# Projection, mask and tile work moved within their steps, and the attention half of the output weights split late

## The chip, the cores and the metric

The kernel runs on one core of a Trainium2 chip. The metric is the device time of one execution in microseconds (us); a measurement gives the median of several runs. The engines are named as the profile names them: PE (matrix multiply; PEld is its weight load), DVE (vector), ACT (scalar), POOL (GpSimd), SP (the queue that issues nearly all DMA transfers here). Each engine works through its own list of instructions in order.

## The reference

One layer of an encoder, for a prompt of 256 tokens and a sample of 2048 tokens (T = 2304 in all), width 1024, all in float32:

```python
h = rms_norm(x, g_pre)
q, k, v, z_a, u_f, z_f = split(h @ w_in)                  # six blocks of 512 columns
y_a = neighbourhood_attention(q, k, v, rpb)               # 8 heads of 64, windows of 8 x 16 cells in rows of 64
y_f = real(fft2(u_f, axes=(seq, group), norm='ortho')) @ w_f + b_f   # 8 groups of 64
mixed = concat([rms_norm(y_a, g_na) * silu(z_a), rms_norm(y_f, g_f) * silu(z_f)])
out = mixed @ w_out
return x + rms_norm(out, g_post)
```

The attention window of a token is clipped at the grid's borders; a table `rpb` gives a bias for each relative place, and what lies outside the window is masked.

## The kernel before, in words

**Products.** Each float32 matrix is split into a high part, rounded to the PE's format, and a low part, the rest. A product is then three matmuls: high by high, high by low, low by high (`mm3`, lines 159 to 162). A split is a pair of instructions: ACT makes the high part, and DVE (sometimes POOL) subtracts it to get the low part, so the low part waits for the high one.

**Stages.** (1) The first projections, v and u of the prompt and of a part of the sample. (2) Sixteen tiles b = 0 to 15 of the prompt's other projections (loop at line 756). (3) `vu(0, ...)`: v and u for the first half of the sample, by a fast multiplication scheme of seven products j = 0 to 6 per tile. (4) Eight pairs of weight blocks, i = 0 to 7, seven products j each (the loop at line 835; one step j is twelve matmuls). (5) `vu(1, ...)`, at i = 8, and i = 8 to 15 for the second half of the sample; along with it the first Fourier stage of u (`u_load`, `u_split`, `u_stage1`). (6) The rest of the Fourier transform. (7) The attention loop, steps k = 2 to 36 (line 1595), over 36 groups G[k]: four head pairs `pr` of nine groups `i` each; and with it the Fourier half of the output product. (8) The attention half of the output product, a loop over 18 token tiles (line 1757).

**What sets the order.** From stage 1 to 5, and again from the Fourier products on, the order of the instructions on every engine is the order of the program text (`manual_schedule`); each engine and the SP queue take them one after another. DMA transfers go through eight completion semaphores in turn, so that a transfer is issued only when the eighth one before it has landed.

**Around the places that are touched.**

- `n_first(j)` (line 425) splits an operand of 128 x 2048 of the scheme's right side; `op_split(j)` (line 466) splits four half tiles of its left side, v's and u's weights. In stage 2 they were called at b = 12, 13 and at b = 14, 15.
- In stage 4 and 5, each step j first prepares weights for the next pair (`w_load`, `w_sums` on POOL, `a_split` on ACT and DVE; what `a_split(i + 1, j)` makes is read seven steps later), then did `n_load`, `n_scale`, `n_diff` (operands for the second half), then `u_load`, `u_split`, `u_stage1`, and then runs the step's twelve matmuls.
- In step k of the attention loop, `scores(g)` puts the scores of G[k] into PSUM; `bias_max` (DVE) adds the bias and takes the extreme; `exps` (ACT) takes the exponential; `soft` (POOL) scales by the reciprocal sum. One step later `transp(f, b)` turns the weights on PE, in two calls b = 0 and 1: it writes two PSUM banks `ptb`, and ACT copies the one, DVE the other to SBUF (`pt`). The second call can only write when both copies of the first have been made. `pv(f)` multiplies by v. `f_mm(k)` is the Fourier half of the output product (PSUM tiles `po`), which `f_evac(k)` takes out into a tile `ofs`, on DVE for even k, on ACT for odd k, and stores to `oD` after the odd one. `split_q(G[k + 1])` (ACT, then POOL) splits the next queries, loaded into `ql` by `prep(G[k + 3])` at the end of step k. `mask_p` (POOL) masks the bias table of the next head pair's first group.
- The attention half of the output weights, `A["wo"][0]`, four blocks of 128 x 1024, is scaled by `gmix` and split. `wo_load` and `wo_split` (lines 701 to 711) did this within `vu(1, ...)` and stored both parts to a tensor `woD` in device memory; steps 24 to 31 of the attention loop loaded the eight results into `WO` (line 1616), which step 36 and stage 8 read.
- The pool behind `gt(...)` (tag `g`) has 13 buffers of 4 KB a partition. In the attention loop eight of them hold the Fourier half of the output weights (`wo1`) until step 35; the others serve `ofs`, and now `wor`.

The lines that order a step of the attention loop, behind the second call of `transp`:

```python
        if g:
            f_mm(k, range(6, 12))
        ...
        if pr < 3 and i == 8:
            mask_p(pr + 1)
        if k % 2 and x < 18:
            ys_split(ftiles[x])
        ...
        if g:
            f_evac(k)
        if f:
            pv(f)
```

Of the kernel before, what the change touches and what calls it, by code (L numbers as in the profile page):

```python
# [164 lines left out]
def build(tc, A, O):  # L165
# [18 lines left out]
    ivD = dr.tile([18, 128], F32, name="ivD")  # L184
    oD = dr.tile([T, D], F32, name="oD")
    yD = dr.tile([2, 4, 128, T], F32, name="yD")
    woD = dr.tile([2, 4, 128, D], F32, name="woD")
    tD = [dr.tile([4, 128, 2, 80 * n], F32, name="tD%d" % n) for n in (11, 15, 12)]

    ident = cst.tile([128, 128], F32, name="ident")  # L190
# [39 lines left out]
    def load(shape, src, name):  # L230
        t = gt(shape, F32, name)
        nc.sync.dma_start(t, src)
        return t
# [464 lines left out]
    for c in range(3):  # L698
        vu_out("u", c)

    def wo_load(x):
        wor[x] = load((128, D), A["wo"][0, x], "wr")

    def wo_split(x):
        w = wor.pop(x)
        g = gmix[:, x:x + 1]
        o = k8(F32R, "wo", (128, 2, D))
        nc.scalar.activation(o[:, 0], w, AF.Copy, scale=g)
        nc.vector.scalar_tensor_tensor(out=o[:, 1], in0=w, scalar=g, in1=f_(o[:, 0]), op0=ALU.mult, op1=ALU.subtract)
        for y in range(2):  # L710
            nc.sync.dma_start(woD[y, x], f_(o[:, y]))

    wor = {}
    for c in range(3, 6):
        if c == 3:
            iv_get(0, 2)
# [39 lines left out]
    for b in range(16):  # L756
        kind, blk = divmod(b, 4)
        if 1 <= b < 10:
            wz_load(1)
        if b == 2:  # L760
            n_load((1, 1))
        if b in (5, 7):
            r_put(b // 2 + 1)
        if b == 10:
            op_load(0)
        if b == 12:
            op_load(1)
        if 2 <= b < 14:
            b_raw(b + 2)
        if 2 <= b < 8:  # L770
            x, y = divmod(b, 2)
            n_scale(None, *divmod(x, 2)[::-1], range(2 * y, 2 * y + 2))
        elif 8 <= b < 12:
            n_sum(b - 8)
        if b in (5, 12, 13):
            n_first((5, 12, 13).index(b) + 1)
        if b > 13:
            op_split(b - 14)
        p = mmt(512)[:, :TP]
        wh, wl = wb.pop(b)  # L780
        for k in range(KC):
            mm3(nc, p, wh[:, k], wl[:, k], hp_[:, k], lp_[:, k], k == 0, k == KC - 1)
        o = st.tile([128, 256], F32, tag="f", name="f", bufs=3)
        if kind % 2:
            i, d = p, o
        else:
            i = p.rearrange("p (b r c) -> p b r c", b=2, c=32)
            d = o.rearrange("p (r b c) -> p b r c", b=2, c=32)
        nc.scalar.activation(d, i, AF.Silu if kind < 2 else AF.Copy)
        if kind < 2:  # L790
            nc.sync.dma_start(zD[kind, blk * 128:blk * 128 + 128, :TP], o)
        else:
            nc.sync.dma_start((kD if kind == 2 else qD)[blk, :, :TP], o)
# [14 lines left out]
    def at(i, f, *a):  # L808
        hooks.setdefault(i, []).append(call(f, *a))

    for x in range(4, 7):
        at(3 * x - 12, n_first, x)
    for x in range(4):
        at(2 * x + 1, rows_load, x + 5)
        at(2 * x + 4, rows_square, x + 5)
# [19 lines left out]
    for i in range(16):  # L835
        sg, pr = divmod(i, 8)
        if i == 8:
            hooks.clear()
            for x in (5, 6):
                at(2 * x - 9, b_split, x)  # L840
            for x in range(4):
                if x:
                    at(4 * x, wo_load, x)
                at(4 * x + 5, wo_split, x)
            at(20, w_load, 8)
            at(24, w_sums, 8)
            for j in range(7):
                at(24 + j // 2, a_split, 8, j)
            vu(1, range(4), hooks)
# [32 lines left out]

        silu_ = [None]
        for j in range(7):
            if i in (0, 8):
                if j in (0, 3):
                    w_load(i + 1 + j // 3)
                if i == 0 and j == 0:
                    a_split(0, 6)
                if i == 0 and j == 1:  # L890
                    row_scales(10, 8)
                if i == 0 and j == 4:
                    iv_rows(10, 8)
                    iv_put(10, 8)
                if i == 0 and j == 6:
                    iv_get(10, 8)
                if j == 2:
                    w_sums(i + 1)
                for x in {3: (0, 1), 4: (2, 3), 5: (4, 5), 6: (6,)}.get(j, ()):
                    a_split(i + 1, x)  # L900
            elif i not in (7, 15):
                if j == 0:
                    w_sums(i + 1)
                a_split(i + 1, j)
                if j == 3 and i < 14 and i != 6:
                    w_load(i + 2)
            elif i == 7:
                if j in (3, 4):
                    op_load(j - 3)
                if j in (5, 6):  # L910
                    op_split(j - 5)
                if j == 5:
                    wo_load(0)
            if sg == 0:
                x, y = divmod(7 * (pr - 1) + j, 14)
                if x in (0, 1):
                    if y == 0:
                        n_load(x)
                    elif 3 <= y < 7:
                        n_scale(x, *divmod(y - 3, 2))  # L920
                    elif 7 <= y < 12:
                        n_diff(x, y - 7)
                if pr == 6 and j in (2, 5):
                    (b_split if j > 2 else b_get)(0)
                if pr == 7 and j:
                    b_get(j)
                    if j > 2:
                        b_split(j - 2)
            if i == 2 and j == 0:
                for t, n in ((gmix, "gmix"), (bfs, "bf"), (dnyq, "dnyq"), (rmask, "rmask"), (csm, "csmask")):  # L930
                    nc.sync.dma_start(t, A[n])
                nc.sync.dma_start(cm, A["cmask"].rearrange("p (b x) -> p b x", b=2))
            for f, d in ((u_load, 0), (u_split, 4), (u_stage1, 6)):
                x = 7 * pr + j - 7 - d
                if sg and 0 <= x < 38 and x % 7 in (2, 4, 6):
                    f(x // 7 * 3 + x % 7 // 2 - 1)
            if i == 5 or 8 <= i < 15:
                t_step(max(0, i - 7), j)
            if i == 15 and j in (1, 3, 4, 5):
                if j == 1:  # L940
                    d2 = [load_d(0), load_d(1)]
                else:
                    zgs.append(load_z(j - 3))
            if 9 <= i < 15 and j == 2:
                v_copy(i - 9)
            p = mmt(512)
            aw = aop[i, j]
            bh, bl = bnew[sg, j]
            for k in range(4):
                mm3(nc, p, aw[:, 0, k], aw[:, 1, k], bh[:, k], bl[:, k], k == 0, k == 3)  # L950
            add = lambda o, u: nc.vector.tensor_tensor(out=e_(o), in0=uu[u], in1=p, op=ALU.add)
            if j == 0:
                nc.scalar.copy(e_("u0"), p)
            elif j == 1:
                comb(0, 0, "u0", p)
            elif j == 2:
                add("u2", "u0")
            elif j == 3:
                add("u4", "u2")
            elif j == 4:  # L960
                comb(1, 1, "u4", p)
                add("u3", "u2")
            elif j == 5:
                comb(1, 0, "u3", p, ALU.subtract)
                store(1)
            else:
                comb(0, 1, "u4", p)
                store(0)
# [596 lines left out]
        if R is None or hc:  # L1565
            nc.sync.dma_start(yD[0, pr, :, ts], y)

    WO = []

    NT = {4: range(2, 4), 8: range(4, 8), 10: range(8, 12), 11: range(12, 16), 12: range(16, 18),  # L1570
          32: range(4), 34: range(4, 8), 36: range(8, 12)}
# [23 lines left out]
    for k in range(2, len(G) + 1):  # L1595
# [12 lines left out]
            load_t(pr, 2)  # L1608
        if k == 9:
            nc.sync.dma_start(gpb, pbc(A["gpost"]))  # L1610
        if k == 23:
            wp = pt.enter_context(tc.tile_pool(name="wp", bufs=1, side="right"))
            WO.extend(wp.tile([128, 4, D], F32R, name="w0%d" % x) for x in range(2))
        if 24 <= k < 32:
            y = k - 24
            nc.sync.dma_start(WO[y % 2][:, y // 2].bitcast(F32), woD[y % 2, y // 2])
        x = k // 2 + 1
        if g:
            scores(g)
# [24 lines left out]
        if g:  # L1644
            if k + 1 < len(G):
                split_q(G[k + 1])
            soft(g, 1)
            if k == 2:
                ys_mul(ftiles[x])
                ys_load(ftiles[x + 1])  # L1650
# [5 lines left out]
            f_mm(k, range(6, 12))  # L1656
        else:
            a_mm(atiles[0], 1, range(6))
        if pr < 3 and i == 8:
            mask_p(pr + 1)  # L1660
        if k % 2 and x < 18:
            ys_split(ftiles[x])
        if pr < 3 and i in (5, 6, 7, 8):
            split_k(KK[pr + 1], i - 5)
        if k == 34:
            ys_split(atiles[0])
        if g:
            f_evac(k)
        if f:
            pv(f)  # L1670
        if k + 1 in NT:
# [15 lines left out]
        if k in (34, 35):  # L1687
            ys_load(atiles[k - 33])
            of_load(atiles[k - 34])
        if k == 36:  # L1690
            ys_split(atiles[1])


    def evac(d, p, ns, q):
# [110 lines left out]
```

## Time and profile before

| | us |
|---|---|
| median of 3 runs | 967.51 (967.21 to 969.06) |
| the profiled execution, its own time | 968.71 |
| span in that profile, first to last instruction | 966.9 |
| PE busy | 957.0 (99% of the span) |
| DVE busy | 710.4 (73%) |
| ACT busy | 496.2 (51%) |
| POOL busy | 429.8 (44%) |
| mean granted TensorE clock | 0.997 |

A row of a timeline has the start and the duration in us, the engine, the line, the operation, out<-in, shapes and the count of instructions merged into it; in brackets stands how long the engine had been idle, and what ended that. A row of the chain of waits has start, duration, and the work that the end of the program depended on. A matmul's duration is longer than the time until the next one may start, since matmuls are pipelined: the distance of the starts tells whether PE waited. The table of stages gives for each stretch its length, and for each engine its busy time with the number of instructions, then the granted clock, the DMA engines' busy share and GB/s.

### The profile page before, as it was taken

How to read it: one execution, taken by the hardware profiler on the slowest of the kernel's cores; microseconds unless marked ns; L12 is line 12 of the kernel's file. 1: busy time of each engine (PE TensorE's matmuls, PEld its weight loads, DVE VectorE, ACT ScalarE, POOL GpSimd, SP SyncE). 2: the span in 40 equal slices, each digit the busy share in tenths (PEclk: the TensorE clock that was granted, in tenths of full speed). 3: DMA queues.
4: the chain of work that ended last, by engine and by line, in shares of the span. 5: the costliest groups of instructions: out<-in, count | busy, mean ns of one | idle time of the engine just before them, and what ended most of it. 6: DMA issues, size and time to landing. Idle time of an engine off the chain costs nothing.

```text
span 966.9 us, 16988 instructions
## 1 busy us (share of the span) xinstructions
PE 957.0 (99%) x5743; PEld 798.7 (83%) x5743; DVE 710.4 (73%) x1310; ACT 496.2 (51%) x1077; POOL 429.8 (44%) x400
## 2 busy tenths in 40 slices
PE   9999999999999999999999999999999999999997
PEld 8889988888888888888887889787787887778886
DVE  6758978687886855798887358776666656649997
ACT  5845676423335432233344267676676766644443
POOL 2200002455752202665655044567677786524544
PEclk9999999999999999999999999999999999999998
DMA  8899696557748893599888895698877998979993
GB/s 304 323 359 374 243 347 244 194 189 276 292 189 358 293 352 117 193 386 335 294 308 319 292 346 208 197 278 280 267 234 245 273 312 260 281 255 333 342 341 130
DMA packets 140942, 269.81 MB, mean 279 GB/s; under 512 B 13402, under 2 KB 81840, under 8 KB 137464
## 3 DMA queue, kind: packets, MB, share of 16 engines
q1 hardware_dynamic: 140360, 268.32, 79.9%
q8 instruction: 46, 0.75, 0.3%
q10 hardware_dynamic: 432, 0.39, 0.1%
q14 instruction: 40, 0.33, 0.1%
q0 software_dynamic: 64, 0.02, 0.0%
HBM read 179.00 MB, written 96.81 MB: 285 GB/s over the span
## 4 chain that ended last, share of the span: by engine, by line
PE 92%; DMA 3%; DVE 1%; SPq 1%; ACT 1%; issue 1%; POOL 1%; DVEq 0%; ACTq 0%; POOLq 0%
PE po L1454 18%; PE mm L161 18%; PE mm L160 17%; PE mm L162 17%; PE pv L1543 5%; PE ptb L1527 5%; PE s L1185 4%; PE pab L1022 2%; DMA wr<-wz 1%; PE py L160 1%; PE py L162 1%; PE py L161 1%; DMA za<-zD 1%; DMA gpre<-gpre 0%; SPq L1153 0%
## 5 line engine op out<-in xcount | busy, mean ns | idle before, releaser
L160 PE MATMUL mm<-xh,wa 128*128 128x512 f32 x448 | 174.4, 389 | 0.0
L162 PE MATMUL mm<-xh,wa 128*128 128x512 f32 x448 | 174.3, 389 | 0.0
L161 PE MATMUL mm<-xl,wa 128*128 128x512 f32 x448 | 174.3, 389 | 0.0
L532 POOL TENSOR_TENSOR ws<-wr 128x512 f32<-128x512 f32 x16 | 23.3, 1455 | 219.9 <-DMA wr<-wz 207.1
L1219 POOL TENSOR_SCALAR w<-w,m 128x465 f32<-128x465 f32 (+9 forms) x136 | 85.2, 638 | 44.0 <-DVE m L1216 33.8
L160 PEld LDWEIGHTS mm<-xh,wa 128*128 128x128 f32 x448 | 84.1, 188 | 17.6
L162 PEld LDWEIGHTS mm<-xh,wa 128*128 128x128 f32 x448 | 84.1, 188 | 17.6
L161 PEld LDWEIGHTS mm<-xl,wa 128*128 128x128 f32 x448 | 84.1, 188 | 17.3
L547 DVE TENSOR_TENSOR wa<-wr,wa 128x512 fp32r<-128x512 f32 x60 | 73.1, 1228 | 26.0 <-ACT wa L546 25.9
L1454 PE MATMUL po<-wo,yh 128*128 128x512 f32 x272 | 90.5, 414 | 0.0
L1212 ACT ACTIVATE w<-w,m 128x465 f32<-128x465 f32 (+9 forms) x136 | 78.3, 579 | 17.0 <-DVE m L1207 16.9
L1454 PE MATMUL po<-w,yh 128*128 128x512 f32 x280 | 86.8, 391 | 0.0
L1207 DVE CUSTOM_DVE_ANT_1 w<-s,tb 128x465 f32<-128x465 f32 (+8 forms) x124 | 61.2, 531 | 10.9 <-PE s L1185 10.4
L161 PE MATMUL mm<-vl,xh 128*128 128x512 f32 x168 | 65.5, 390 | 0.2 <-DVE vl L478 0.2
L160 PE MATMUL mm<-vh,xh 128*128 128x512 f32 x168 | 65.4, 389 | 0.0
L162 PE MATMUL mm<-vh,xl 128*128 128x512 f32 x168 | 65.4, 389 | 0.0
L585 POOL TENSOR_TENSOR mt<-mt,rmask 128x880 f32<-128x880 f32 (+2 forms) x24 | 50.3, 2110 | 31.6 <-DVE mt L581 25.1
L873 DVE TENSOR_TENSOR f<-u,mm 128x512 f32<-128x512 f32 x64 | 43.4, 678 | 27.1 <-PE mm L162 22.4
L1454 PEld LDWEIGHTS po<-w,yh 128*128 128x128 f32 x280 | 52.1, 188 | 11.2 <-issue 0.4
L546 ACT CAST wa<-wr 128x512 fp32r<-128x512 f32 x60 | 36.4, 617 | 44.5 <-PE mm L162 22.8
L1527 PE MATMUL ptb<-ident,w 128*120 128x128 f32 (+8 forms) x422 | 58.9, 276 | 0.1
L1543 PEld LDWEIGHTS pv<-pt,v 120*64 120x64 f32 (+9 forms) x880 | 47.5, 136 | 13.9 <-issue 9.9
(265 smaller groups left out, 2390.0 us busy)
## 6 DMA issues: line engine op xcount, KB each, us to landing
wr<-wz SPq DMA_DIRECT2D x48, 512.0 KB
vl<-sD SPq DMA_DIRECT2D x20, 512.0 KB
xm<-xm SPq DMA_DIRECT2D x9, 1024.0 KB
oD<-ofs SPq DMA_DIRECT2D x18, 512.0 KB
of<-oD SPq DMA_DIRECT2D x18, 512.0 KB
yr<-yD SPq DMA_DIRECT2D x34, 256.0 KB
zD<-f SPq DMA_DIRECT2D x16, 512.0 KB
xD<-nx SPq DMA_DIRECT2D x14, 512.0 KB
```

Source lines behind the costliest of these rows:

```text
L160: nc.tensor.matmul(out, lh, rh, start=first, stop=False)
L161: nc.tensor.matmul(out, lh, rl, start=False, stop=False)
L162: nc.tensor.matmul(out, ll, rh, start=False, stop=last)
L547: nc.vector.tensor_tensor(out=o[:, 1], in0=src, in1=o[:, 0].bitcast(F32), op=ALU.subtract)
L585: nc.gpsimd.tensor_tensor(out=o, in0=i, in1=rmask[:, m0:m0 + n].unsqueeze(2).to_broadcast([128, n, 80]), op=ALU.add)
L873: nc.vector.tensor_tensor(out=dst(f, b), in0=src(uu[u]), in1=src(p), op=op)
L1207: nc.vector.tensor_tensor_reduce(out=rows(g["w"][b][:, h, :n], w), in0=rows(g["s"][2 * b + h][:, :nr * sw(w)], sw(w))[:, :, :w], in1=tv, s ...
L1212: nc.scalar.activation(w, w, AF.Exp, bias=m[:, h:h + 1], scale=-1.0, accum_out=m[:, 2 + h:3 + h])
L1219: nc.gpsimd.tensor_scalar(w, w, m[:, 4 + h:5 + h], 1.0, ALU.mult, ALU.mult)
L1454: nc.tensor.matmul(p, (d["l"] if x == 2 else d["h"])[:, c], w(n, int(x == 1), c), start=j == 0, stop=j == 11)
L1527: nc.tensor.transpose(ptb[h][:nk, j * 128:j * 128 + 128], g["w"][b][:, h, c0:c0 + nk], ident)
L1543: nc.tensor.matmul(p[hs, b], g["v"][:nk, v, hs], g["pt"][b][:nk, h, j * 128:j * 128 + 128], start=j == 0, stop=j == len(ch) - 1)
```

## The change

Four things.

1. In stage 2 `op_split(0)` comes a tile earlier (b = 13) and `n_first(3)` a tile later (b = 14); in `vu(0, ...)` `n_first(4), (5), (6)` come at tiles 0, 3 and 8, in place of 0, 3 and 6.
2. In each step j of stages 4 and 5 `u_load`, `u_split`, `u_stage1`, then `n_load`, `n_scale`, `n_diff` come ahead of the weights' preparation. On PE nothing moves.
3. In the attention loop `mask_p` comes ahead of `soft(g, 1)`, and in step 36 the split of the second attention tile comes ahead of `pv(f)`.
4. `woD`, `wo_load`, `wo_split` and the eight loads of steps 24 to 31 go. Steps 27 to 30 load the four blocks as they are, each into a buffer `wor` of the pool behind `gt`; steps 30, 32, 34 and 35 split one block each, ACT and DVE, directly into `WO`. The pool of `WO` is opened at step 21 in place of 23.

```diff
-    woD = dr.tile([2, 4, 128, D], F32, name="woD")
...
-    def wo_load(x):
-        wor[x] = load((128, D), A["wo"][0, x], "wr")
-
-    def wo_split(x):
-        w = wor.pop(x)
-        g = gmix[:, x:x + 1]
-        o = k8(F32R, "wo", (128, 2, D))
-        nc.scalar.activation(o[:, 0], w, AF.Copy, scale=g)
-        nc.vector.scalar_tensor_tensor(out=o[:, 1], in0=w, scalar=g, in1=f_(o[:, 0]), op0=ALU.mult, op1=ALU.subtract)
-        for y in range(2):
-            nc.sync.dma_start(woD[y, x], f_(o[:, y]))
...
-        if b in (5, 12, 13):
-            n_first((5, 12, 13).index(b) + 1)
-        if b > 13:
-            op_split(b - 14)
+        if b in (5, 12, 14):
+            n_first((5, 12, 14).index(b) + 1)
+        if b in (13, 15):
+            op_split((b - 13) // 2)
...
-        at(3 * x - 12, n_first, x)
+        at((0, 3, 8)[x - 4], n_first, x)
...
-            for x in range(4):
-                if x:
-                    at(4 * x, wo_load, x)
-                at(4 * x + 5, wo_split, x)
...
         for j in range(7):
+            for f, d in ((u_load, 0), (u_split, 4), (u_stage1, 6)):
+                x = 7 * pr + j - 7 - d
+                if sg and 0 <= x < 38 and x % 7 in (2, 4, 6):
+                    f(x // 7 * 3 + x % 7 // 2 - 1)
+            x, y = divmod(7 * (pr - 1) + j, 14)
+            if sg == 0 and x in (0, 1):
+                if y == 0:
+                    n_load(x)
+                elif 3 <= y < 7:
+                    n_scale(x, *divmod(y - 3, 2))
+                elif 7 <= y < 12:
+                    n_diff(x, y - 7)
             if i in (0, 8):
...
-                if j == 5:
-                    wo_load(0)
...
-        if k == 23:
+        if k == 21:
             wp = pt.enter_context(tc.tile_pool(name="wp", bufs=1, side="right"))
...
-        if 24 <= k < 32:
-            y = k - 24
-            nc.sync.dma_start(WO[y % 2][:, y // 2].bitcast(F32), woD[y % 2, y // 2])
+        if 27 <= k < 31:
+            wor[(30, 32, 34, 35)[k - 27]] = w = gt([128, D], F32, "wor")
+            nc.sync.dma_start(w, A["wo"][0, k - 27])
...
+            if pr < 3 and i == 8:
+                mask_p(pr + 1)
             soft(g, 1)
...
-        if pr < 3 and i == 8:
-            mask_p(pr + 1)
         if k % 2 and x < 18:
             ys_split(ftiles[x])
+        if k in wor:
+            w, c = wor.pop(k), (30, 32, 34, 35).index(k)
+            nc.scalar.activation(WO[0][:, c], w, AF.Copy, scale=gmix[:, c:c + 1])
+            V.scalar_tensor_tensor(out=WO[1][:, c], in0=w, scalar=gmix[:, c:c + 1], in1=f_(WO[0][:, c]),
+                                   op0=ALU.mult, op1=ALU.subtract)
...
         if g:
             f_evac(k)
+        if k == 36:
+            ys_split(atiles[1])
         if f:
             pv(f)
...
-        if k == 36:
-            ys_split(atiles[1])
```

(The old places of `u_load` to `u_stage1` and of `n_load` to `n_diff`, further down in the same step, go; they are left out above.)

More of the change, by code (lines that the diff above doesn't have):

```diff
@@ L699, in build @@
         vu_out("u", c)
-    def wo_load(x):
-        wor[x] = load((128, D), A["wo"][0, x], "wr")
-    def wo_split(x):
-        w = wor.pop(x)
-        g = gmix[:, x:x + 1]
-        o = k8(F32R, "wo", (128, 2, D))
-        nc.scalar.activation(o[:, 0], w, AF.Copy, scale=g)
-        nc.vector.scalar_tensor_tensor(out=o[:, 1], in0=w, scalar=g, in1=f_(o[:, 0]), op0=ALU.mult, op1=ALU.subtract)
-        for y in range(2):
-            nc.sync.dma_start(woD[y, x], f_(o[:, y]))
-    wor = {}
     for c in range(3, 6):
@@ L911, in build @@
                     op_split(j - 5)
-                if j == 5:
-                    wo_load(0)
             if sg == 0:
[L915 to L922, printed above, removed]
                 if pr == 6 and j in (2, 5):
@@ L932, in build @@
                 nc.sync.dma_start(cm, A["cmask"].rearrange("p (b x) -> p b x", b=2))
[L933 to L936, printed above, removed]
             if i == 5 or 8 <= i < 15:
@@ L1566, in pv @@
             nc.sync.dma_start(yD[0, pr, :, ts], y)
-    WO = []
+    WO, wor = [], {}
     NT = {4: range(2, 4), 8: range(4, 8), 10: range(8, 12), 11: range(12, 16), 12: range(16, 18),
```

## The prediction

> **What bounds the kernel now.** I read the page first: busy shares, then the chain of work that ended last.
>
> ```profile
> span 966.9 us, 16988 instructions
> PE 957.0 (99%) x5743; PEld 798.7 (83%) x5743; DVE 710.4 (73%) x1310; ACT 496.2 (51%) x1077; POOL 429.8 (44%) x400
> PE 92%; DMA 3%; DVE 1%; SPq 1%; ACT 1%; issue 1%; POOL 1%; DVEq 0%; ACTq 0%; POOLq 0%
> ```
>
> PE is busy for 99% and carries 92% of the chain. The change moves no instruction on PE, so it can only change the stalls that PE has. Next comes the table of stages, for the stretch that holds the old split of the output weights and for the attention loop:
>
> ```profile
> 300.00:325.00 25.00, 25.00 (x112) 20.67 (x111) 21.68 (x14) 16.73 (x14) 10.71 (x2) 1.00 0.94 359
> 775.00:800.00 25.00, 25.00 (x235) 20.70 (x232) 15.09 (x54) 16.69 (x51) 20.95 (x28) 1.00 1.00 319
> 800.00:825.00 25.00, 24.75 (x220) 19.50 (x219) 14.63 (x46) 15.55 (x46) 15.82 (x24) 1.00 0.84 256
> ```
>
> In the first row 112 matmuls fill 25.00 us, one each 0.223 us, at clock 1.00: no stall. That spacing is the measure for the four places where the timeline of PE shows a stall at a line the change touches:
>
> ```profile
> 119.14 0.39 PE L160 MATMUL mm<-vh,xh 128*128 128x512 f32 x1
> 119.74 0.50 PE L161 MATMUL mm<-vl,xh 128*128 128x512 f32 x1 [0.21 <-DVE vl L478]
> ...
> 511.51 0.39 PE L160 MATMUL pz<-ut,f1h 128*128 128x512 f32 x1
> 512.34 0.50 PE L161 MATMUL pz<-ut,f1h 128*128 128x512 f32 x1 [0.44 <-DVE ut L368]
> ...
> 730.46 0.40 PE L1454 MATMUL po<-wo,yl 128*128 128x512 f32 x1
> 730.93 0.29 PE L1527 MATMUL ptb<-ident,w 128*96 128x128 f32 x1
> ...
> 864.74 0.73 PE L1454 MATMUL po<-w,yh 128*128 128x512 f32 x2
> 865.60 0.50 PE L1454 MATMUL po<-w,yl 128*128 128x512 f32 x1
> ```
>
> Start to start less 0.223 (twice that for the x2 row, with 0.1 of unevenness taken off) gives stalls of 0.37, 0.60, 0.24 and 0.3 us. What was late, on DVE and POOL:
>
> ```profile
> 116.27 2.28 DVE L429 TENSOR_TENSOR xl<-nx,xh 128x2048 fp32r<-128x2048 f32 x1
> 118.47 4.62 DVE L478 TENSOR_TENSOR vl<-vr,vh 128x1024 fp32r<-128x1024 f32 x4
> ...
> 508.97 1.62 DVE L547 TENSOR_TENSOR wa<-wr,wa 128x512 fp32r<-128x512 f32 x1 [1.63 <-ACT wa L546]
> 510.51 1.77 DVE L368 TENSOR_TENSOR ut<-ut 128x512 fp32r<-128x512 f32 x1
> ...
> 729.53 0.32 DVE L1207 CUSTOM_DVE_ANT_0 w<-s,tb 128x160 f32<-128x160 f32 x1 [1.23 <-POOL tb L1114]
> ...
> 864.72 0.83 DVE L1445 TENSOR_TENSOR yl<-yr,yh 128x512 fp32r<-128x512 f32 x1 [1.02 <-ACT yh L1440]
> ```
> ```profile
> 727.95 1.55 POOL L1114 TENSOR_TENSOR tb<-cm,tb 128x640 f32<-128x640 f32 x1
> ```
>
> Each stall has its operand late by the work just ahead of it.
>
> **The change part by part.** *Projections (part 1).* With the first `op_split` a tile ahead of `n_first(3)`, the `vl` of 118.47 no longer stands behind the 2.28 us `xl`; a start at 116.3 has the first of its four 1.16 us pieces ready 2.2 us sooner, and PE wanted it 0.37 us sooner. −0.37. `n_first(3)` now stands between the two `op_split`s; it takes the place that the first left, and the four pieces together end when they did (near 123.1). The move of `n_first(6)` from tile 6 to 8 falls into stage 3, where the 25 us rows show no stall: 0.
>
> *Steps of stages 4 and 5 (part 2).* `u_split` ahead of `a_split`: `ut` need not follow the 1.62 us `wa` that waited 1.63 for ACT. It would end 1.6 us sooner, near 510.7, before 511.74 where PE would have taken it. −0.60. What falls behind instead is `wa`, read seven steps (7 × 12 × 0.223 = 18.7 us) later; a delay of 2 us is covered by that distance. The u loads go ahead of the weights' loads on SP by a position or two; the same distance covers it. The `u_split`s of the other steps showed no stall, and gain 0.
>
> *Mask and tile (part 3).* The mask comes ahead of a POOL `soft` of about 1.4 us, so the bias that waited 1.23 for it starts about that much sooner, and the 0.24 goes, with some 0.07 of the like at step 9. `soft`'s result is then ready 1.55 later, near 729.5, and PE wants it at the transposes of 730.7 (730.93 less the stall): covered by 1.2 us; if it is not, the transposes stall by what is missing. −0.30. In step 36 the tile's split ahead of `pv` frees the 864.72 `yl`: −0.30; the y operations that now follow it by 0.83 feed no matmul until stage 8.
>
> The four make −1.57.
>
> *The old split of the weights (part 4).* Going: four loads, eight stores and these, all in `vu(1, ...)`:
>
> ```profile
> L708 ACT ACTIVATE wo<-wr,gmix x4: 1147/1150/1157, 328.6 to 351.1; 128x1024 fp32r<-128x1024 f32 x4
> L709 DVE SCALAR_TENSOR_TENSOR wo<-wr,gmix,wo x4: 1276/1276/1278, 330.5 to 357.3; 128x1024 fp32r<-128x1024 f32 x4
> ```
>
> 4 × 1.15 of ACT and 4 × 1.28 of DVE lie beside a full PE (the 300 to 325 row): worth 0. Four loads of 512 KB fewer in the loop too: those of steps 24, 25, 26 and 31.
>
> *The new split.* The same 1.15 and 1.28 now stand at the head of ACT and DVE in steps 30, 32, 34 and 35, ahead of `f_evac`, `pv`'s y and the next step's `bias_max`. These rows price it:
>
> ```profile
> 815.83 0.40 ACT L1164 CAST qh<-ql 128x256 fp32r<-128x256 f32 x1 [1.89 <-DMA ql<-qD]
> 832.74 0.40 ACT L1164 CAST qh<-ql 128x256 fp32r<-128x256 f32 x1 [2.89 <-DMA ql<-qD]
> 846.21 0.41 ACT L1164 CAST qh<-ql 128x256 fp32r<-128x256 f32 x1
> ```
> ```profile
> 814.71 0.75 DVE L1486 TENSOR_SCALAR ofs<-po,invf 128x512 f32<-128x512 f32 x1 [0.77 <-PE po L1454]
> ...
> 816.18 0.42 DVE L1557 TENSOR_TENSOR y<-pv,za 128x256 f32<-128x256 f32 x1 [0.72 <-PE pv L1543]
> 817.62 0.64 DVE L1207 CUSTOM_DVE_ANT_1 w<-s,tb 128x465 f32<-128x465 f32 x1 [1.01 <-PE s L1185]
> 819.21 0.55 DVE L1531 COPY pt<-ptb 120x384 f32<-120x384 f32 x1
> ...
> 834.53 0.65 DVE L1207 CUSTOM_DVE_ANT_1 w<-s,tb 128x465 f32<-128x465 f32 x1 [0.86 <-PE s L1185]
> ...
> 849.60 0.55 DVE L1207 CUSTOM_DVE_ANT_1 w<-s,tb 128x372 f32<-128x372 f32 x1 [0.29 <-PE s L1185]
> ```
> ```profile
> 820.10 1.03 PE L1527 MATMUL ptb<-ident,w 128*120 128x128 f32 x8
> 837.02 1.03 PE L1527 MATMUL ptb<-ident,w 128*120 128x128 f32 x8
> 851.97 0.82 PE L1527 MATMUL ptb<-ident,w 128*128 128x128 f32 x6
> ```
> ```profile
> 812.60 0.38 SPq L1484 DMA_DIRECT2D oD<-ofs  x1
> ```
>
> Step 30: ACT stands 1.89 us idle for the queries `ql` until 815.83, and the split's high part waits behind that cast: 816.2 to 817.3, then the low part to 818.6. `f_evac` comes next. Its tile `ofs` now has to wait for the store issued at 812.60, since four raw blocks hold the pool's other free buffers; I estimate its landing near 819.15, when SP got on after it. So `ofs` ends near 819.8, y at 820.2, and the biases start there rather than at 817.62; the copy of 819.21 ends at 822.3 where the transposes began at 820.10: 2.2 us late. Step 32: cast 832.74, split 833.1 to 834.3 and to 835.55, `ofs` and y to 836.6, 2.1 later than the bias at 834.53. The copy before 837.02 had 0.4 to spare: about 1.6 late. Step 34: cast 846.21, split to 849.0, then `yl`, `ofs` and y to 850.7, 1.1 later than 849.60, and 0.6 of room: +0.45. Step 35's splits wait for no load and fit: 0.
>
> The lateness at 30 and that at 32 need not add, because between them PE has stalls of its own to give back:
>
> ```profile
> 831.23 1.99 PE L1543 MATMUL pv<-pt,v 120*64 120x128 f32 x28 [0.74 <-DVE dt L1405]
> ```
> ```profile
> 829.90 1.20 DVE L1405 TENSOR_TENSOR dt<-dy 128x4 f32<-128x4 f32 x1
> 846.37 0.14 DVE L1405 TENSOR_TENSOR dt<-dy 128x4 f32<-128x4 f32 x1
> ```
> ```profile
> 829.80 1.27 POOL L1431 TENSOR_TENSOR yr<-yr,yz 128x512 f32<-128x512 f32 x1 [3.88 <-DMA yz<-zD]
> ```
>
> PE's 0.74 comes of a late load, for which POOL stood idle 3.88 us. If the loads keep their times, only the lateness at 32 against the old clock stays.
>
> Do they keep them? Each 512 KB takes 1.6 us at the 319 GB/s of the 775 row and 2.0 at the 256 of the 800 row. From 775 to 800 the DMA engines are at 1.00, so the three loads gone before step 27 free up to 4.9 us there; after 800 the share is 0.84, so by 816 some 2.5 us passed unused, and the queue was then held by something other than bytes. The loads of `ql` come sooner by 0 to 2.5 us; I take 1.1, near the middle. Then step 30 is 1.1 late, which the vanishing stalls give back, and step 32 is 0.5 late.
>
> Sum: −1.57 + 0.5 + 0.45 = −0.62. The profiled execution took 968.71 by its own time (span 966.9), 1.2 above the median of 967.51; so 968.1 by its measure and 966.9 as a median.
>
> *A rule against it.* The low part of the split reads two tensors in SBUF, as `dt` does. `dt` of four columns took 1.20 us beside the POOL row of 829.80 and 0.14 alone.
>
> The Trainium skill, "SBUF — State Buffer", section "SBUF: two separate sides", says that such a DVE operation and a GpSimd operation that reads SBUF share a pair of ports, which the first holds for its whole instruction; the trace agrees by 1.20 against 0.14. By that rule each low part may stand for the rest of a POOL instruction, half of 1.27 us as an estimate, and at steps 32 and 34 that is on the path: the sum would be +0.7 by the rule in place of −0.6 by the rows alone.
>
> **The rivals.** *The loads do not move.* For it: at 800 to 825 DMA is at 0.84, so bytes do not set the times. Then step 32 is 1.6 late: −1.57 + 1.6 + 0.45 = +0.5, median 968.0. Against it: the 1.00 share in the row before.
>
> *Slower: the delays of 30 and 32 add.* The loads are issued as engines free buffers; a split that holds DVE by 2.2 us at step 30 then holds back the next loads too, and `ql` of step 32 comes 2.2 later. −1.57 + 2.2 + 1.6 + 0.45 = +2.7, median 970.2. It decides (over +1.9) once the two together reach 3.1 us, that is from a cast at step 32 later than about 834.2, against 832.74 now. For it: the cast at 832.74 waited 2.89, longer than the one at 815.83, so the queue was not recovering. Against it: the DMA share has 0.16 to recover by.
>
> *Faster: the queue catches up.* With the 4.9 us freed, the late loads of steps 30 to 33 come in time: the 0.74 goes, and the two casts' waits (1.89, 2.89), which I estimate at 0.8 of PE together, go too. Then step 30 costs 0.15, 32 nothing: −1.57 − 0.74 − 0.8 + 0.15 + 0.45 = −2.5, median 965.0. For it: the 1.00 share. Against it: 0.84 after.
>
> The Trainium skill, "Perfetto Trace Analysis", section "Summary: the profiler window per engine type", says that the profiled window of a DMA instruction holds the issue and not the movement of data; no row here shows one transfer's movement by itself, so 819.15 stays an estimate.
>
> **How the numbers follow.** About 0.2%, 1.9 us, is what a measurement of this kernel can tell from no change. Chances: forecast 0.38 (966.9), loads unmoved 0.22 (968.0), delays add 0.20 (970.2), queue catches up 0.20 (965.0). Below 965.6 lies the last, and 0.02 of the forecast's: faster 0.22. Above 969.4 lies the third, and 0.01 of the second's: slower 0.21. The rest, 0.57, is no change. The range reaches from 964.8 to 970.3 and leaves out the lower third of the last case and half of the third.
>
> **What would show it.** Right: no gap before the four matmuls of 119.74, 512.34, 730.93 and 865.60; no rows of `woD`; `ofs` of step 30 waiting for a DMA; ACT's cast at steps 30 and 32 a microsecond sooner; transposes of steps 32 and 34 about 0.5 late each. Wrong: the casts at step 32 later than 834.2 and larger gaps before the transposes (slower), or no wait for `ql` at all in steps 30 to 33 (faster); a `wa` or `soft` that PE waits for, if a cover of parts 2 and 3 is gone.

## The result and the profile after

The changed kernel takes 970.38 us in the median of 7 runs (969.93 to 973.5), the kernel before 967.51 (7 runs beside it, 967.14 to 969.06): 1.0035 times as long, 95% interval 1.0024 to 1.0046. It is slower; the forecast was 966.9 and no change, and 970.38 lies just above the range.

The page of the changed kernel, with the lines that answer to those of before (the lines of the code stand 1 to 20 lower in it than before):

```profile
span 968.2 us, 16970 instructions
PE 954.9 (99%) x5743; PEld 797.7 (82%) x5743; DVE 705.5 (73%) x1310; ACT 496.6 (51%) x1077; POOL 435.2 (45%) x400
PE 78%; DVE 2%; DMA 1%; ACT 1%; issue 1%; POOL 1%; DVEq 0%; SPq 0%; ACTq 0%; POOLq 0%
```

PE executes as many matmuls as before, and the span is 1.3 us longer; the loss is again in PE's stalls. (The medians lie 2.9 apart: before's profiled execution was 1.2 above its median, this one, 969.97, 0.4 below.) The timeline of PE at the places where the prediction expected stalls to go, and at those where there are new ones:

```profile
118.78 0.40 PE L160 MATMUL mm<-vh,xh 128*128 128x512 f32 x1
119.02 0.40 PE L161 MATMUL mm<-vl,xh 128*128 128x512 f32 x1
...
151.45 0.39 PE L160 MATMUL mm<-vh,xh 128*128 128x512 f32 x1
152.61 0.50 PE L161 MATMUL mm<-vl,xh 128*128 128x512 f32 x1 [0.77 <-DVE vl L477]
...
153.87 0.40 PE L160 MATMUL mm<-vh,xh 128*128 128x512 f32 x1
154.85 0.50 PE L161 MATMUL mm<-vl,xh 128*128 128x512 f32 x1 [0.58 <-DVE vl L477]
...
264.85 0.39 PE L162 MATMUL mm<-xh,wa 128*128 128x512 f32 x1
266.69 0.50 PE L160 MATMUL mm<-xh,wa 128*128 128x512 f32 x1 [1.45 <-ACT u L933]
...
514.34 0.39 PE L160 MATMUL pz<-ut,f1h 128*128 128x512 f32 x1
514.57 0.39 PE L161 MATMUL pz<-ut,f1h 128*128 128x512 f32 x1
...
588.84 0.41 PE L160 MATMUL py<-abh,pqh 128*128 128x384 f32 x1 [1.45 <-DVE Y L1274]
```

At 118.78 and 514.34 the next matmul follows after 0.23 or 0.24: those two stalls are gone. New are 0.93 at 152.61, 0.75 at 154.85, 1.61 at 266.69 and 1.62 at 588.84. A table says it for whole stages: for each matmul the time since the one before it, less the shortest such time in any of the fourteen profiles of this case, summed over a stage. The column of stage 2 goes on to 130 us and holds the stall of 119.74. It is one execution for each kernel, so a figure holds only where several kernels agree.

| profile (us of stall) | stage 2 | stage 3 | stage 4 | vu(1), stage 5 | Fourier | attention loop |
|---|---|---|---|---|---|---|
| before | 0.81 | 0.14 | 0.41 | 1.41 | 0.58 | 5.12 |
| changed | 0.27 | 2.06 | 2.16 | 0.68 | 2.34 | 2.54 |
| e2, n_ pieces back | 0.29 | 1.48 | 0.41 | 0.68 | 1.16 | 2.52 |
| e1, n_first(6) back | 0.31 | 0.76 | 7.17 | 0.68 | 0.80 | 2.90 |
| e5, both back | 0.29 | 0.73 | 2.11 | 0.73 | 1.66 | 2.51 |
| e3, late split alone | 0.76 | 0.11 | 0.41 | 1.00 | 0.79 | 3.49 |
| e7, n_ pieces ahead alone | 0.84 | 0.11 | 4.94 | 1.23 | 0.38 | 3.05 |
| e11, n_diff ahead alone | 0.80 | 0.11 | 5.25 | 1.13 | 0.99 | 3.30 |

Surprisingly, the attention loop, where the prediction put its whole loss, has become better by 2.6 us, and stages 3 and 4, where it put nothing, lose 3.7 (the Fourier stage 1.8, see what stays open).

**Stage 4, around 266.69.** SP of the kernel before, then of the changed one:

```profile
243.79 9.19 SPq L404 DMA_DIRECT2D xD<-nx  x5
253.07 1.20 SPq L232 DMA_DIRECT2D wr<-wz  x2
255.46 3.13 SPq L404 DMA_DIRECT2D xD<-nx  x2
```
```profile
245.51 14.20 SPq L403 DMA_DIRECT2D xD<-nx  x6
259.75 1.25 SPq L231 DMA_DIRECT2D wr<-wz  x2
261.85 0.33 SPq L403 DMA_DIRECT2D xD<-nx  x1
```

`n_diff` is a POOL operation and a store of its result (its first call is three stores alone). With `n_diff` ahead of `w_load` in the step, six stores and no longer five stand ahead of the weights' loads on SP. SP issues in order, and a store waits until POOL has made what it stores. POOL of the kernel before, then POOL and ACT of the changed one:

```profile
247.40 5.23 POOL L408 TENSOR_TENSOR nx<-nx 128x1024 f32<-128x1024 f32 x2 [0.39 <-DMA xD<-nx]
```
```profile
249.17 2.78 POOL L407 TENSOR_TENSOR nx<-nx 128x1024 f32<-128x1024 f32 x1 [6.35 <-DVE u L931]
251.92 1.74 POOL L531 TENSOR_TENSOR wr<-wr,ws 128x512 f32<-128x512 f32 x1
253.62 8.20 POOL L407 TENSOR_TENSOR nx<-nx 128x1024 f32<-128x1024 f32 x3
```
```profile
265.53 0.63 ACT L548 ACTIVATE wa<-wr 128x512 fp32r<-128x512 f32 x1 [11.22 <-DMA wr<-wz]
266.06 0.57 ACT L933 COPY u<-mm 128x512 f32<-128x512 f32 x1
```

The third `nx` is made near 259.1 (253.62 and two of 2.73), and then the loads can go, at 259.75, 6.7 us later than before's 253.07, which followed the second `nx`. Besides the third `nx`, a piece of the weights' sums (`wr`, 1.74) now stands between the first and the second. ACT waits 11.22 us with the split of these weights at its head; behind it stands the copy of the PSUM tile that PE needs, and PE stands still. The split's result was not wanted for seven steps, but the copy behind it was wanted at once. Before, ACT and PE had the same work like this, without a stall:

```profile
257.97 0.64 ACT L549 ACTIVATE wa<-wr 128x512 fp32r<-128x512 f32 x1 [6.89 <-DMA wr<-wz]
258.51 0.57 ACT L953 COPY u<-mm 128x512 f32<-128x512 f32 x1
```
```profile
264.00 0.39 PE L160 MATMUL mm<-xh,wa 128*128 128x512 f32 x1
```

That matmul is the one of 266.69. Before, the copy ended at 259.08, 4.92 ahead of it. In the changed kernel the copy is 7.55 later and PE comes 1.07 later (264.85 and one spacing against 264.00): 7.55 − 4.92 − 1.07 = 1.56, against a stall of 1.61.

**Stage 3, around 152.61.** DVE before, then DVE and POOL of the changed kernel:

```profile
145.60 2.35 DVE L474 SCALAR_TENSOR_TENSOR vl<-vl,vh 128x1024 fp32r<-128x1024 f32 x2
...
150.26 2.35 DVE L478 TENSOR_TENSOR vl<-vl,vh 128x1024 fp32r<-128x1024 f32 x2
```
```profile
146.73 2.29 DVE L428 TENSOR_TENSOR xl<-nx,xh 128x2048 fp32r<-128x2048 f32 x1 [2.65 <-ACT xm L294]
...
151.33 3.46 DVE L477 TENSOR_TENSOR vl<-vl,vh 128x1024 fp32r<-128x1024 f32 x2
```
```profile
152.42 1.29 POOL L531 TENSOR_TENSOR ws<-wr 128x512 f32<-128x512 f32 x1 [124.92 <-DMA wr<-wz]
153.79 2.15 POOL L531 TENSOR_TENSOR ws<-ws,wr 128x512 f32<-128x512 f32 x1
```

`n_first(6)`, now at tile 8, stands between two `op_split`s; its `xl` waits 2.65 us for ACT's squares (it did so too at its old place, 2.67, where the `vl` behind it was ready at 146.81 and PE took it at 147.09, only 0.28 later). The last `vl` starts 1.07 later, PE comes to it some 0.9 sooner (it was 0.36 sooner already at 118.78, and the stall of 119.74, 0.37, is gone), and beside the POOL sums its two pieces take 3.46 and not 2.35. The first two make the stall of 0.93, the longer second piece that of 0.75.

### The profile page after: what moved, and what is told of

It is laid out like the page before. It is cut to its first block, busy times and chain, and to the rows that moved or that the text cites. A ratio compares the mean times of both kernels' runs of the same rounds, so it can differ in the third digit from the quotient of the medians.

```text
span 968.2 us, 16970 instructions
## 1 busy us (share of the span) xinstructions
PE 954.9 (99%) x5743; PEld 797.7 (82%) x5743; DVE 705.5 (73%) x1310; ACT 496.6 (51%) x1077; POOL 435.2 (45%) x400
## 4 chain that ended last, share of the span: by engine, by line
PE 78%; DVE 2%; DMA 1%; ACT 1%; issue 1%; POOL 1%; DVEq 0%; SPq 0%; ACTq 0%; POOLq 0%
PE po L1434 20%; PE mm L161 13%; PE mm L162 13%; PE mm L160 13%; PE pv L1523 5%; PE ptb L1507 5%; PE s L1165 4%; PE pab L1002 2%; DMA wr<-wo 1%; PE py L160 1%; POOL nx L407 1%; DMA wr<-wz 1%; PE py L162 1%; PE py L161 1%; PE ppq L1040 0%
## 5 line engine op out<-in xcount | busy, mean ns | idle before, releaser
L1199 POOL TENSOR_SCALAR w<-w,m 128x465 f32<-128x465 f32 (+9 forms) x136 | 87.7, 657 | 43.3 <-DVE m L1196 35.3
L1511 DVE COPY pt<-ptb 120x384 f32<-120x384 f32 (+5 forms) x72 | 40.5, 563 | 25.7 <-PE ptb L1507 25.6
```

Source lines behind the costliest of these rows:

```text
L1199: nc.gpsimd.tensor_scalar(w, w, m[:, 4 + h:5 + h], 1.0, ALU.mult, ALU.mult)
L1511: V.tensor_copy(o[:z, h, :n], ptb[h][:z, :n])
```

## The experiments

Theory A: the loss comes of two moves to which the prediction gave nothing, `n_first(6)` and the `n_` pieces. Theory B: it comes of the late split. All experiments were timed against the kernel before on the same chip; its median there was 967.1 to 967.4.

**e1, n_first(6) back.**

```diff
-        at((0, 3, 8)[x - 4], n_first, x)
+        at((0, 3, 6)[x - 4], n_first, x)
```

> The changed kernel with n_first(6) back at tile 6 of stage 3; all else as changed. Theory A (two of the moved pieces cost: n_first(6) at tile 8, and n_scale and n_diff ahead of the weights): the two gaps of PE at 152.61 and 154.85, 0.89 and 0.75 us, go, nothing else moves: about 968.7 against 970.4. Theory B (the late splits of the output weights cost what the kernel lost, and the gaps before 300 us only move): no change, 970.4.

Measured: 972.76 (968.94 to 975.48), 1.0051 (1.0033 to 1.0068). Neither. The two gaps of stage 3 are gone, but stage 4 loses more:

```profile
245.86 0.47 PE L160 MATMUL mm<-xh,wa 128*128 128x512 f32 x1 [0.72 <-DVE f L855]
...
269.06 0.50 PE L160 MATMUL mm<-xh,wa 128*128 128x512 f32 x1 [3.90 <-ACT u L933]
```

The wait of stage 4 is not a fixed price. PE was 0.17 us ahead of the changed kernel at 246, but the weights' loads were issued at 261.93, 2.2 later than there. The lag is older: ACT's cast of 168.96 waits for a weights' load (167.64 in the changed kernel), DVE's `nx` of 191.72 for its own (189.30 there), and the engines keep a lag of 1.7 to 2.7 up to 246. Why those loads landed later is open. And the stall of 4.06 is not the whole price: the matmuls behind it run at half the rate (see e11), which adds 1.7.

**e2, n_load, n_scale and n_diff back** behind the weights' preparation; the u work stays ahead.

> The changed kernel with n_load, n_scale and n_diff back behind the preparation of the weights; u_load, u_split and u_stage1 stay ahead of it. Theory A: SP no longer holds the weights' loads behind stores that wait for POOL, and the gap of 1.62 us at 266.69 goes: about 968.7 against 970.4. Theory B: no change, 970.4.

Measured: 968.32, 1.0012 (1.0002 to 1.0022). As theory A says: stage 4 shows no gap, and `wr` comes in time. Stage 3 still has one (1.24 at 153.39).

**e3, the late split alone** (part 4 on the kernel before).

> The kernel before with part 4 alone: no woD, raw blocks loaded in steps 27 to 30, splits in steps 30, 32, 34 and 35. Theory A: the splits cost at most some 0.3 us at step 34 and the loads that are gone take away the late loads of steps 30 to 33: 966.0 to 967.5, not slower than before. Theory B: 0.95 us or more slower than before, 968.5 to 970.2, with gaps before the second transposes of steps 30, 32 and 34.

Measured: 966.84 (966.22 to 967.51), 0.9994 (0.9986 to 1.0003). Not slower: theory B falls.

**e4, the four moves** that the prediction priced at a gain, on the kernel before.

> The kernel before with the four moves that the prediction priced at a gain: op_split ahead of n_first(3), u_load to u_stage1 ahead of the weights, the mask ahead of soft, the tile's split ahead of pv in step 36. n_first(6), n_scale and n_diff and the output weights stay as before. The prediction's step: 1.57 us faster, 965.9. Rival: the gap of 1.45 us at 588.84 of the changed kernel comes with the move of the u work, and eats the gain: 967.4, with that gap in the trace.

Measured: 966.25, 0.9990 (0.9977 to 1.0002); no more than a hint of the 1.57. The profiled run was the slowest of its runs, 970.47, so its gaps (1.86 at 246.98, 0.93 at 587.44) need not be typical. It also has a new gap of 0.83 at 147.14, on the `vl` of `op_split(5)` behind `n_first(6)`, after the one at 119.74 has gone: the cover of 0.28 there is less than what PE has gained. The rival's gap near 588 is there in part (0.93 of 1.62), but e1 and e8 have the same u move without it (0.80 and 0.47 in the whole stage).

**e5, both pieces back**: e1 and e2 together.

> The changed kernel with n_first(6) back at tile 6 and n_load, n_scale and n_diff back behind the weights' preparation: the four moves of e4 and the late split together. Theory A (the store of n_diff that SP now takes ahead of the weights' loads made the loss): no gap near 266, 965.8 to 966.5, that is e4's 966.25 and e3's 0.3 gain, faster than before's 967.1. Theory C (any of the moves of part 1 loses, since e1 lost more with n_first(6) back): 968 to 972, with gaps of PE between 147 and 270 us.

Measured: 965.76 (964.53 to 967.95), 0.9984 (0.9975 to 0.9993): faster than both kernels. Its profiled run, the slowest of its eleven, has no gap near 266, but 0.47 at 146.72 and 1.60 at 246.32, where theory C looked for gaps. With e1, e2 and the changed kernel this makes a square, in ratios to before:

| | n_ pieces back | n_ pieces ahead |
|---|---|---|
| n_first(6) at tile 6 | 0.9984 (e5) | 1.0051 (e1) |
| n_first(6) at tile 8 | 1.0012 (e2) | 1.0035 (changed) |

The one move costs 0.28% by itself, the other 0.67%, and both together 0.51%, clearly less than their sum of 0.95% (that it is less than the second alone lies within the intervals). The profiles offer a reason: with `n_first(6)` late PE comes later to the matmul that waits, its stall there is 1.61 and not 4.06, and no slow matmuls follow.

**e6, the weights' loads first.** The changed kernel, with `w_load` alone ahead of `n_diff` in steps j = 3, so that SP has its old order and POOL and DVE the new one.

> The changed kernel with one pair of DMA issues moved: in the steps j = 3 the two loads of the weights come ahead of n_diff and its store, so that SP has its old order; ACT, DVE and POOL keep the changed order. Theory A1 (SP's order alone makes the gap of 266.69): the loads are issued some 5 us sooner, the gap goes, 968.3 as in e2. Theory A2 (POOL's order, nx ahead of the last piece of the weights' sums, makes it): the gap stays, 970.4 or more.

Measured: 969.57, 1.0023 (1.0014 to 1.0031). Between the two, and beside e2's 1.0012 and the changed kernel's 1.0035 about half of the loss is won back, though the intervals of neighbours overlap. The gap goes from 1.61 to 0.40:

```profile
250.04 11.63 SPq L403 DMA_DIRECT2D xD<-nx  x5
261.71 1.26 SPq L231 DMA_DIRECT2D wr<-wz  x2
```
```profile
268.21 0.50 PE L160 MATMUL mm<-xh,wa 128*128 128x512 f32 x1 [0.24 <-ACT u L933]
```

The size of that gap proves little, for in this execution stage 3 lost 3.3 us and PE came there 2.7 later than in the changed kernel. But counted from the first `nx` (254.32 here) the loads are issued 7.39 later, against 10.58 in the changed kernel and 5.67 before. So SP's order makes 3.2 of the 4.9 us, and the other 1.7 is the piece of the weights' sums, which POOL still makes between its first two `nx`.

**e7, the n_ pieces ahead, alone**, on the kernel before.

> The kernel before with one move alone: n_load, n_scale and n_diff ahead of the weights' preparation. Theory A: a gap of 1.6 us or more near 264 us of before, 968.7 to 970.0 against 967.1. Rival (the gap needs the other moves, which bring PE there sooner): 967.1.

Measured: 971.40 (968.67 to 975.34), 1.0040 (1.0026 to 1.0055): slower by about as much as the whole change, with 2.76 us of stall at 266.50. The move needs no other to lose.

**e11, n_diff ahead, alone**; `n_load` and `n_scale` stay.

> The kernel before with n_diff alone ahead of the weights' preparation; n_load and n_scale stay behind it. Theory A (one store on SP and one operation on POOL more ahead of the weights make the loss): as e7, 0.4% over before, 971. Rival (n_scale on DVE ahead of the weights' splits makes it): as before, 967.2.

Measured: 972.14 (971.49 to 973.26), 1.0055 (1.0043 to 1.0067). SP and PE:

```profile
246.50 14.23 SPq L404 DMA_DIRECT2D xD<-nx  x6
260.82 1.21 SPq L232 DMA_DIRECT2D wr<-wz  x2
```
```profile
264.06 0.39 PE L162 MATMUL mm<-xh,wa 128*128 128x512 f32 x1
267.30 0.50 PE L160 MATMUL mm<-xh,wa 128*128 128x512 f32 x1 [2.85 <-ACT u L954]
...
268.83 0.63 PE L162 MATMUL mm<-xh,wa 128*128 128x512 f32 x1
269.26 0.63 PE L160 MATMUL mm<-xh,wa 128*128 128x512 f32 x1
```

The six stores in 14.23 us and the late `wr` are the changed kernel's; of the three pieces it is `n_diff`. The last two rows show a second price, which the changed kernel's profile does not have: from 268.4 to 271.4 the matmuls start 0.43 apart and not 0.23, and the granted clock is 0.50 from 269 to 271. That adds 1.75 to the stall of 3.01, together 4.76; the medians differ by 4.77. The same follows the stalls of 2.76 in e7 (1.8 more) and 4.06 in e1 (1.7 more), and does not follow the changed kernel's 1.61 or 2.15 in stage 3 of e6.

**e10, n_first(6) late, alone**, on the kernel before.

> The kernel before with one move alone: n_first(6) at tile 8 of stage 3 in place of 6. By e2 against e5 it costs 0.28%, 2.7 us: 969.9 against 967.2, with gaps of PE near 153 us at j = 6's first low parts. Rival (it only costs with op_split ahead of n_first(3), which brings PE there sooner): 967.2, or less by the gap that it takes away at 147.

Measured: 968.58, 1.0021 (1.0012 to 1.0030): it costs by itself, some 2 us. The profiled run was among its fastest (967.73) and shows 0.49 at 152.70; there the two pieces of the late `vl` take 2.35, and the second gap is missing.

**e8, without part 1.** On the kernel before: the u work, the mask, the tile's split and the late split.

> The kernel before with the u work ahead of the weights, the mask ahead of soft, the tile's split ahead of pv and the late split; nothing of part 1, n_load to n_diff as before. By the prediction's terms 0.60, 0.30 and 0.30 go: 965.9 with e3's 966.84 less the part of it that e3 has already, and no gap between 120 and 300 us beyond before's 0.37 at 119.74. Theory C: the same, since nothing of part 1 is in it; a time over 967.5 would say that the u work's move loses.

Measured: 966.04, 0.9986 (0.9976 to 0.9996). So part 1's gain of 0.37 can't be seen in the time (e5 with it: 0.9984). But one expectation fails: a gap of 0.88 at 147.65, on the `vl` of `op_split(5)`, in a kernel whose engines run the same instructions in the same order as before's up to 299 us. Five of the kernels show it (0.47 to 1.37, e1, e4, e5, e8, e12), all with `n_first(6)` at its old place. The traces tell how it comes about, though no run tried it: before, this `vl` is ready 0.28 ahead of PE; in e8 it is 0.79 later (146.38 against 145.60), behind loads of `vl` that landed later, and in e5 PE would take it at 146.25, 0.84 sooner than before. So what part 1 gains at 119.74 it mostly gives back at 147, unless `n_first(6)` moves too, and then 152 has the stall.

**e9, four loads more.** On e3:

```diff
+        if k in (24, 25, 26, 31):
+            nc.sync.dma_start(gt([128, D], F32, "dm"), A["wo"][0, k % 4])
```

> e3 (the kernel before with the late split alone) with four more loads of 512 KB into free buffers of the pool, in steps 24, 25, 26 and 31, where the kernel before loaded from woD; nothing reads them. Theory L (the bytes of the four loads that went were what made the queries late): the casts of qh in steps 30 and 32 wait for a DMA again, and with the splits behind them the second transposes of steps 30 and 32 come late: 0.5 to 2 us over e3, 967.4 to 968.8. Rival (the late loads of before's profile were that execution's): no wait, 966.8.

Measured: 970.16 (5 runs, 968.43 to 971.77), 1.0038 (1.0025 to 1.0051): more than 3 us over e3. The profiled run was its fastest; DVE, PE and the table of stages there:

```profile
817.42 0.75 DVE L1466 TENSOR_SCALAR ofs<-po,invf 128x512 f32<-128x512 f32 x1 [0.44 <-DMA oD<-ofs]
```
```profile
820.38 1.06 PE L1507 MATMUL ptb<-ident,w 128*120 128x128 f32 x8 [0.50 <-ACT pt L1509]
```
```profile
775.00:800.00 25.00, 25.00 (x237) 20.71 (x234) 15.25 (x54) 16.52 (x50) 21.44 (x28) 1.00 1.06 337
```

Here `ofs` of step 30 does wait for the store of step 28, behind the low part of the split, and the second transposes of step 30 come 0.66 late: nearly the chain that the prediction drew (the copy that PE waits for is ACT's, behind the exponential, and not DVE's), brought about by the loads. The casts of `qh` do not wait in this run, so that part of the expectation was not seen; what the slower runs of e9 wait for has no profile.

**e12, the third split in step 33**, on e5.

> e5 with the third split in step 33 in place of 34. If the 0.37 us gap of PE before the second transposes of step 34 is all that the splits cost, and step 33 has room for one as step 35 has: 0.4 us less than e5, 965.4. If step 33, where ACT also takes out ofs, has no room: a gap there, 965.8 or more.

Measured: 966.66, 0.9997 (0.9988 to 1.0006); 0.77 of stall before the second transposes of step 33:

```profile
843.48 1.09 PE L1507 MATMUL ptb<-ident,w 128*120 128x128 f32 x8 [0.70 <-ACT nsb L1483]
```

Step 33 has no room; step 34 with 0.38 is the better place.

## Why the prediction was wrong, point by point

**The step that failed** is part 2, "Steps of stages 4 and 5". It looked at `u_split` and `wa` on DVE and at the u loads on SP, and said of what falls behind that "the same distance covers it". `n_load`, `n_scale` and `n_diff`, in the same hunk, were not costed at all. One store of `n_diff` and one POOL operation came ahead of the weights' loads; e11 has that alone at 1.0055, and e2 without the three at 1.0012. Two errors lie in it. A cover was reckoned from when the result is read (18.7 us later), where the split's wait holds up ACT at once, with PE's copy behind it: the cover was 4.92 us, and the copy came 7.55 later. And the store was not asked what it waits for. The page of before had a row that could have warned:

```profile
L532 POOL TENSOR_TENSOR ws<-wr 128x512 f32<-128x512 f32 x16 | 23.3, 1455 | 219.9 <-DMA wr<-wz 207.1
```

POOL waited 207.1 us in all for just these loads. 123.31 of that is one wait at 153.67, for the first of them, so the sum alone doesn't say what is short; the nearer sign is ACT's row of 257.97 above, which waited 6.89 for such a load with PE's copy behind it.

**A second step failed**: "The move of `n_first(6)` from tile 6 to 8 falls into stage 3, where the 25 us rows show no stall: 0." The 25 us row it points to is of 300 to 325 us, and that there was no stall says nothing about how near one was: `vl` of 150.26 had its first piece ready near 151.4, and PE took it at 152.55:

```profile
152.55 0.39 PE L161 MATMUL mm<-vl,xh 128*128 128x512 f32 x1
```

The cover was 1.1 us. The move alone costs 0.21% (e10), 0.28% beside the other moves (e2 against e5).

**Parts 1 and 3 and the u work**: three stalls went as drawn, at 119, 512 and 865; the mask's too, 0.24 (the shift between the two kernels falls by that there). Three of them have the same size in every profile of a kernel with the old order (0.37, 0.24, 0.30). The 0.60 at 512 was in part that execution's: the five other profiles with the old order have 0.08 to 0.42. And the `vl` of 147 takes the 0.37 back (0.47 of stall there in e5; see e8). Together with the late split they give 0.9984 in e5, 1.6 us. That this is near the sum of 1.57 is luck: the gains of four moves were less (e4: 0.9 us, 0.9990), and the late split, forecast as a loss, has no part in that sum.

**The late split** was forecast at +0.95 and costs 0.38, the gap at step 34, where 0.45 had been drawn:

```profile
853.87 0.85 PE L1507 MATMUL ptb<-ident,w 128*128 128x128 f32 x6 [0.22 <-ACT pt L1509]
```

At steps 30 and 32 it costs nothing, for the loads are in time:

```profile
817.23 0.41 ACT L1144 CAST qh<-ql 128x256 fp32r<-128x256 f32 x1
825.08 0.41 ACT L1144 CAST qh<-ql 128x256 fp32r<-128x256 f32 x1
832.69 0.41 ACT L1144 CAST qh<-ql 128x256 fp32r<-128x256 f32 x1
```

No row has a wait, where before's had 1.89 and 2.89. That is what the rival "the queue catches up" forecast. Of the five profiles with the old loads four have such waits (e11 has none), of the nine with the late split none. From 775 to 800 the DMA share is 0.88 in place of 1.00:

```profile
775.00:800.00 25.00, 25.00 (x228) 20.68 (x229) 14.62 (x49) 17.74 (x52) 21.65 (x29) 1.00 0.88 282
```

e9, with four loads back, has 1.06 there and loses over 3 us against e3. So these loads have a price, and the shift of 1.1 us that I took was too small. That bytes alone made the queries late is not shown: e9's casts do not wait.

**The rival that ended slower** (delays of 30 and 32 add, 970.2) has the measured time, but not its mechanism: those delays are not there.

**The rule on the ports.** The Trainium skill, "SBUF — State Buffer", section "SBUF: two separate sides", by which the operation that starts first holds the shared ports for its whole instruction, stood behind the prediction's second sum, +0.7. There I let a low part wait for half a POOL instruction, an estimate of mine. The four low parts took 1.29 to 1.44 us against 1.28 before, up to 0.16 more, so as a price for this place my half was four times too high:

```profile
L1646 DVE SCALAR_TENSOR_TENSOR w<-wor,gmix,w x4: 1285/1399/1439, 818.7 to 856.8; 128x1024 fp32r<-128x1024 f32 x4
```

In stage 3 the same rule agrees with the trace better: `vl` beside POOL's sums took 3.46 for two, 1.11 more, its second piece having begun just behind a POOL sum of 1.29. In e2 the sum of 153.65 began while a piece of `vl` ran; there the sum took 1.98 in place of 1.29, and the pair of `vl` its 2.35.

**What stays open.** Why the loads of 168 and 191 land later in e1 than in the changed kernel. The stall near 246 (0.88 in e1, 1.86 in e4, 1.60 in e5, 1.01 in e6, 1.06 in e12), where DVE's `f` is late: five of the seven kernels with `op_split` ahead of `n_first(3)` have it, none of the seven others, and no run tried which piece brings it. The 1.62 at 588.84: ACT waited there 4.13 us for a load of the Fourier half of the weights with the PSUM copies behind it; seven other kernels with the u work ahead have 0.47 to 1.85 in that stage, six without it 0.38 to 0.99, and none was made to tell it apart. And how much of before's 5.12 in the attention loop is that execution's: its run was 1.2 above the median, and the four others with the old loads have 3.05 to 4.39.

## What to carry to other kernels

Moving a step ahead moves its DMA issues ahead too: for each, ask what it waits for, and which loads stand behind it on the issuing queue. A result that is read late is not therefore free to come late: the instruction that waits for its input holds its engine, and the price is that of the next instruction there. A long stall can cost more than its length: here 3.0 us of it brought 1.75 more at a granted clock of 0.50. A stage without stalls can have none because an operand comes 1.1 us early, or 0.28, so look for how early each operand is before something is put ahead of it.

## What the runs showed of the hardware

In one stage PE stood still for 2.76, 3.01 and 4.06 us (e7, e11, e1); each time its matmuls then ran 0.43 us apart for some 3 us at a granted clock of 0.50, and back at 0.23 after that. After 1.61 (changed) and 2.15 (e6) they did not.

Where a two-input DVE operation and a POOL sum met, the one that began later took longer: the piece of `vl` by 1.11 in the changed kernel (152.47 against the sum's 152.42), the sum of 153.65 by 0.69 in e2.

The same kernel's executions differ by up to 0.7% here (968.94 to 975.48 in e1, 968.67 to 975.34 in e7). In these two kernels the 12 executions with a mean granted clock of 0.996 or less took 970.43 to 975.48, the 8 others 968.67 to 974.68, five of them below 970. So a single profile says where a stall can be, and only the medians what it costs.
